# Mixer A's queries and keys turned by transposing DMA transfers of half-word planes instead of TensorE

## The chip, the core and the metric

The kernel runs on one core of one Trainium2 chip. The core has five engines that work side by side, each through its own list of instructions in order: TensorE (PE; matrix products and transposes, results in PSUM), VectorE (DVE), ScalarE (ACT), GpSimd (POOL) and SyncE (SP), which here only issues DMA transfers. They meet through semaphores: an instruction waits until another engine or a transfer has counted far enough. The metric is the device time of one run, in microseconds (us); lower is better. The kernel before takes 1428.91 us (median of 3 runs, 1428.28 to 1428.96).

## What is computed

A two-layer encoder trunk on 512 positions of width 1024, float32. Layer 1 uses mixer A, dilated window attention, layer 2 uses mixer B, latent attention; each is followed by a squared-ReLU MLP of width 4096. What matters here is the front of mixer A: one projection gives queries, keys and values for 3 groups of 8 heads of width 128; queries and keys are RMS-normalised per head and rotated, and then each group takes scores inside its window.

```
def dilated_mixer(h, w_qkv, q_gain, k_gain, w_o):
    qkv = (h @ w_qkv).reshape(B, S, 3, N_GROUPS, A_HEADS, A_HEAD_DIM)
    for g, (window, dil) in enumerate(DIL_CONFIGS):
        q = rope(rms_norm(qkv[:, :, 0, g], q_gain[g]), S)
        k = rope(rms_norm(qkv[:, :, 1, g], k_gain[g]), S)
        v = qkv[:, :, 2, g]
        o, lse = dilated_group(q, k, v, window, dil)
    ...
def reference(x, ...):
    for i in range(DEPTH):
        y = dilated_mixer(...) if i % 2 == 0 else mla_mixer(...)
        x = x + y
        x = x + sq_relu_mlp(rms_norm(x, norm_ffn[i]), ffn_w1[i], ffn_w2[i])
```

The score of a query and a key is a sum over the head's 128 columns. TensorE sums over partitions, so queries and keys must lie with the head's columns on the partitions, while the projection leaves them with the positions there. They have to be transposed in between.

## The kernel before

The 512 positions are cut into 4 chunks of 128 (r = 0 to 3; a chunk holds every fourth position). Mixer A goes over 4 head pairs b, and within each over the groups g = 0, 1, 2. One pair and group make a block: 512 projected columns (two heads of queries, two of keys) for each of the 4 chunks, so there are 12 blocks and 48 chunks.

*Projection.* `qk_proj` runs `run_block` over 8 slices of 128 rows of the weights. Float32 products are made of three matmuls of split operands: `load_unit` reads a weight tile `raw` (L145), ScalarE rounds it to `whi` (L157), VectorE makes the rest `wlo` (L158), and L185 multiplies. Four PSUM banks `acc` hold the four chunks. `raw` has 3 buffers, `whi` and `wlo` 4 each.

*A finished chunk.* `qk_evac` squares the four heads' columns with their sums on ScalarE (L137, `junk` and `qss`), multiplies by cosines into `t1` (L277) and by sines into `t2` (L280), raises the sums to the power -1/2 on GpSimd (L132, `qrs`), adds `t2` to `t1` (L285) and scales `t1` (L286). Then TensorE transposes the four 128x128 pieces of `t1` into one PSUM bank `tp` (L124), and ScalarE copies that bank into `qkT` (L295): into a contiguous slice for groups 1 and 2, into every fourth column for group 0. `t1`, `t2`, `tp` and `qkT` have two buffers each.

*After it.* `scores` (L576, L580, L587) multiplies slices of `qkT`; VectorE adds the mask and takes the maxima (L583, L592, L595, L596), ScalarE takes the exponentials (L598); `merge` weighs the three groups and `pv` multiplies with the values.

*What sets the order.* The code issues blocks one after the other, but the instructions of each engine are put in order by the framework's scheduler when the program is built, from its own estimate of times; on the chip each engine then keeps that order. The order therefore changes in many places of mixer A when the code of one step changes. SP's list holds loads of weights, of the values (`vt`, `v0n`, `v0c`) and of a few constants in this stage.

The lines that the change touches are L263 to L301 (`qk_evac`, `qk_proj`) and L711 to L716 (`project_in`).

Of the kernel before, what the change touches and what calls it, by code (L numbers as in the profile page):

```python
# [9 lines left out]

F32 = mybir.dt.float32
F32R = mybir.dt.float32r
AF = mybir.ActivationFunctionType
ALU = mybir.AluOpType
AX = mybir.AxisListType
# [2 lines left out]
P = 128  # L18
S = 512
NT = S // P  # L20
# [67 lines left out]
def encoder_kernel(ctx: ExitStack, tc: tile.TileContext, x, norm_mix, norm_ffn, a_w_qkv, a_q_gain, a_k_gain,  # L88
                   a_w_o, b_w_in, b_q_a_gain, b_w_qb, b_kv_a_gain, b_w_kvb, b_q_gain, b_k_gain, b_w_o,
                   ffn_w1, ffn_w2, consts, out):  # L90
    nc = tc.nc
    V, A, G, PE = nc.vector, nc.scalar, nc.gpsimd, nc.tensor
# [3 lines left out]
    def nm(s):  # L96
        uid[0] += 1
        return f"{s}_{uid[0]}"
# [14 lines left out]
    tp_p = ctx.enter_context(tc.tile_pool(name="tp_p", bufs=2, space=PSUM))  # L113
# [6 lines left out]
    ident = ck[:, C_ID:C_ID + P]  # L120
    A.activation(warm, nhalf[:, 0:1], AF.Exp)

    def transpose(o, i):
        PE.transpose(o, i, ident)  # L124

    def rstd_of(ss, n, add, name, out=None):

        v = st.tile([P, 8], F32, tag="rs_v", name=nm("rs_v"))
        V.tensor_scalar(v[:, :n], ss, add, None, op0=ALU.add)  # L129
        if out is None:  # L130
            out = st.tile([P, 8], F32, tag=name, name=nm(name))[:, :n]
        G.tensor_tensor(out, v[:, :n], nhalf[:, :n], op=ALU.pow)  # L132
        return out

    def mean_square(junk, x, dim, out):

        A.activation(junk, x, AF.Square, scale=1.0 / math.sqrt(dim), accum_out=out)  # L137

# [11 lines left out]
    def load_unit(src, nk, dims, n, home=None, raw=None):  # L150
# [3 lines left out]
        if home is None:  # L154
            home = [wp.tile([P, 2, 512], F32R, tag=t, name=nm(t)) for t in ("whi", "wlo")]
        hi, lo = home
        A.activation(hi[:, :nk, :n], raw[:, :nk, :n], AF.Copy)  # L157
        V.tensor_tensor(lo[:, :nk, :n], raw[:, :nk, :n], hi[:, :nk, :n].bitcast(F32), op=ALU.subtract)  # L158
# [36 lines left out]
    def run_block(units, groups, n, mm, evac, outs=NT, halves=1):  # L195
        for end in block_groups(units, groups, n, mm, outs, halves):
            if end is not None:
                evac(*end)

    def act_stationary(hT, n):  # L200

        def mm(r, kt, hi, lo, hv):
            ah = hT[:, kt, 0, r * P:(r + 1) * P]
            al = hT[:, kt, 1, r * P:(r + 1) * P]
            sl = slice(0, n)
            return [(ah, hi[:, :n], sl), (ah, lo[:, :n], sl), (al, hi[:, :n], sl)]
        return mm
# [6 lines left out]
    def norm_tile(r, src, gain_b, hT, pool, xn_bufs=2, xn_tag="xn"):  # L214
# [6 lines left out]
        for half in range(2):  # L221
# [5 lines left out]
            tv = tp.rearrange("p (k t) -> p k t", k=4)  # L227
            A.activation(hi, tv, AF.Copy)
            V.tensor_tensor(lo, tv, hi.bitcast(F32), op=ALU.subtract)
# [6 lines left out]
    def new_hT():  # L236
        return big.tile([P, KD, 2, S], F32R, tag="hT", name=nm("hT"))

# [6 lines left out]
    def qk_units(b, g):  # L245
        return [(w6[:, k:k + 2, 0:2, g, 256 * b:256 * b + 256], 2, 2) for k in range(0, KD, 2)]
# [9 lines left out]
    def tables(g, gqk, cos, sin):  # L256

        for t in range(2):
            gb = gqk[:, t].rearrange("p (f d) -> p f d", f=2).unsqueeze(1).broadcast_to([P, NT, 2, 64])
            V.tensor_tensor(cosg[g][:, :, t].rearrange("p r (f d) -> p r f d", f=2),  # L260
                            cos.rearrange("p (r d) -> p r d", r=NT).unsqueeze(2).broadcast_to([P, NT, 2, 64]), gb,
                            op=ALU.mult)
            V.tensor_tensor(sing[g][:, :, t].rearrange("p r (f d) -> p r f d", f=2),  # L263
                            sin.rearrange("p (r f d) -> p r f d", r=NT, f=2), gb, op=ALU.mult)

    def qk_evac(g, qkT, r, acc, homes, junk):

        a4 = acc.rearrange("p (c d) -> p c d", c=4)
        a5 = acc.rearrange("p (t h d) -> p t h d", t=2, h=2)
        ss = st.tile([P, 8], F32, tag="qss", name=nm("qss"))  # L270
        jk = junk()
        for c in range(4):
            mean_square(jk, a4[:, c], DH, ss[:, c:c + 1])
        t1, t2 = homes()
        t15 = t1.rearrange("p (t h) d -> p t h d", t=2)
        t25 = t2.rearrange("p (t h) d -> p t h d", t=2)
        V.tensor_tensor(t15, a5, cosg[g][:, r].unsqueeze(2).broadcast_to([P, 2, 2, DH]), op=ALU.mult)  # L277
        for hf in range(2):
            o_ = 64 - hf * 64
            V.tensor_tensor(t25[:, :, :, hf * 64:hf * 64 + 64], a5[:, :, :, o_:o_ + 64],  # L280
                            sing[g][:, r, :, o_:o_ + 64].unsqueeze(2).broadcast_to([P, 2, 2, 64]), op=ALU.mult)
        rs = rstd_of(ss[:, 0:4], 4, EPS, "qrs")

        def end():
            V.tensor_tensor(t1, t1, t2, op=ALU.add)  # L285
            V.tensor_tensor(t1, t1, rs.unsqueeze(2).broadcast_to([P, 4, DH]), op=ALU.mult)  # L286
            tp = tp_p.tile([P, 512], F32, tag="tp", name=nm("tp"))
            for c in range(4):
                transpose(tp[:, c * P:(c + 1) * P], t1[:, c])
            tv = tp.rearrange("p (c t) -> p c t", c=4)  # L290
            if g == 0:
                dst = qkT.rearrange("p c (m r) -> p c m r", r=NT)[:, :, :, r]
            else:
                dst = qkT[:, :, r * P:(r + 1) * P]
            A.activation(dst, tv, AF.Copy)  # L295
        return end

    def qk_proj(b, g, qkT, homes, junk):

        run_block(qk_units(b, g), [2, 2], 512, act_stationary(hT, 512),  # L300
                  lambda r, acc: qk_evac(g, qkT, r, acc, homes, junk)())  # L301

    def load_gains(g, gqk):
        for t, src in enumerate((a_q_gain, a_k_gain)):
# [2 lines left out]
    def v_phase(vp):  # L307
# [10 lines left out]
        xts = x16.tile([P, NT, D], F32, tag="x16", name="xts")  # L318
        Ssp = [vp.tile([P, 4, 2, 256], F32R, name=f"Ssp{n}") for n in range(4)]

# [42 lines left out]
        def turn(r):  # L363

            i = r % 2
            for half in (1, 0):
# [5 lines left out]
                hi, lo = (hT[:, sl, c, r * P:(r + 1) * P] for c in range(2))  # L372
                A.activation(hi, tv, AF.Copy)
                V.tensor_tensor(lo, tv, hi.bitcast(F32), op=ALU.subtract)
# [28 lines left out]
        def split_w(x):  # L403
            hi = wp.tile([P, 2, 512], F32R, tag="whi", name=nm("whi"))[:, :, :VH]
            lo = wp.tile([P, 2, 512], F32R, tag="wlo", name=nm("wlo"))[:, :, :VH]
            A.activation(hi, x, AF.Copy)
            V.tensor_tensor(lo, x, hi.bitcast(F32), op=ALU.subtract)  # L407
            return hi, lo
# [135 lines left out]
    with tc.tile_pool(name="apool", bufs=1, reuse_waits="tile") as ap_, \  # L544
# [160 lines left out]
        def homes():  # L705
            return [aw.tile([P, 4, DH], F32, tag=t, name=nm(t)) for t in ("t1", "t2")]

        def junk():
            return aw.tile([P, P], F32, tag="junk", name=nm("junk"), bufs=1)

        def project_in(b, g):  # L711
            if b == 0 and g:
                tables(g, gqk[:, g - 1], ca[:, 0:256], ca[:, 256:768])
            qkT = aw.tile([P, 4, S], F32, tag="qkT", name=nm("qkT"))
            qk_proj(b, g, qkT, homes, junk)
            return qkT  # L716

        def finish(b, Pt, stats, vs):
# [3 lines left out]


        qkT = project_in(0, 0)
        for b in range(HA // 2):
            Pt = [[ap_.tile([P, NT, 256 if g == 0 else P], F32, tag=f"P{g}{h}", name=nm("P")) for h in range(2)]
                  for g in range(NG)]
            stats = [st.tile([P, NG, 2, NT], F32, tag=f"stat{j}", name=nm("stat"), bufs=2) for j in range(3)]
            vs = v_load(b)
            for g in range(NG):  # L730
                scores(b, g, qkT, Pt, stats)
                if g + 1 < NG:
                    qkT = project_in(b, g + 1)
            if b + 1 < HA // 2:
                qkT = project_in(b + 1, 0)
                finish(b, Pt, stats, vs)
# [18 lines left out]
    def split_a(x, pool):  # L755
        t = pool.tile([P, 4, 2, 256], F32R, tag="asp", name=nm("asp"), bufs=4)
        A.activation(t[:, :, 0], x, AF.Copy)
        V.tensor_tensor(t[:, :, 1], x, t[:, :, 0].bitcast(F32), op=ALU.subtract)
        return t
# [191 lines left out]
    if True:  # L951
        with tc.tile_pool(name="bpool", bufs=1, reuse_waits="tile") as bp, \
# [208 lines left out]
            for s_ in range(HB * NT + lag):  # L1161
                p, c = divmod(s_, 8)
# [4 lines left out]
                if s_ >= lag:  # L1167
                    d, h2, r2, f = pend.pop(0)
# [58 lines left out]
```

## Time and profile before

| | before |
|---|---|
| median of 3 runs | 1428.91 us |
| span of the profiled execution, first to last instruction | 1425.8 us |
| VectorE busy | 939.6 us, 66% |
| GpSimd busy | 217.2 us, 15% |
| bytes moved by DMA | 185.25 MB |

The profiled execution's own time is its span; the medians are of other runs and include some us around the span. The profile names an instruction by its line, engine, operation, and output and input tiles (`qkT<-tp`). "Busy" is time in which the engine executes. PEld is the loading of TensorE's weights, which overlaps its products. The chain that ended last is followed back from the last instruction to what released it, and so on. In a row of a group, the numbers behind the first bar are busy us and mean ns, those behind the second the idle time just before the instructions, with what ended most of it. SPq stands for SP's queue of DMA issues.

### The profile page before, as it was taken

How to read it: one execution, taken by the hardware profiler on the slowest of the kernel's cores; microseconds unless marked ns; L12 is line 12 of the kernel's file. 1: busy time of each engine (PE TensorE's matmuls, PEld its weight loads, DVE VectorE, ACT ScalarE, POOL GpSimd, SP SyncE). 2: the span in 40 equal slices, each digit the busy share in tenths (PEclk: the TensorE clock that was granted, in tenths of full speed). 3: DMA queues.
4: the chain of work that ended last, by engine and by line, in shares of the span. 5: the costliest groups of instructions: out<-in, count | busy, mean ns of one | idle time of the engine just before them, and what ended most of it. 6: DMA issues, size and time to landing. Idle time of an engine off the chain costs nothing.

```text
span 1425.8 us, 19234 instructions
## 1 busy us (share of the span) xinstructions
PE 1394.0 (98%) x7044; PEld 1183.8 (83%) x7044; DVE 939.6 (66%) x1497; ACT 740.5 (52%) x1594; POOL 217.2 (15%) x240
## 2 busy tenths in 40 slices
PE   7999999999999999999999999999999999999998
PEld 7999888988888988888888887777768888888886
DVE  6886768676886754465564759788745365575647
ACT  6554656464564623553545446677633553544543
POOL 1110212021112001020010203433201020020201
PEclk9999999999999999999999999999999999999999
DMA  9535222322322335668493844200115658394835
GB/s 323 166 134 168 75 87 87 107 89 75 118 61 77 121 134 195 174 133 222 116 233 99 206 120 91 82 31 30 44 40 163 183 127 231 93 234 128 192 90 118
DMA packets 121086, 185.25 MB, mean 130 GB/s; under 512 B 8416, under 2 KB 58336, under 8 KB 120992
## 3 DMA queue, kind: packets, MB, share of 16 engines
q1 hardware_dynamic: 101808, 144.96, 31.6%
q0 software_dynamic: 19184, 39.07, 15.2%
q8 instruction: 55, 0.90, 0.3%
q14 instruction: 39, 0.32, 0.1%
HBM read 176.13 MB, written 7.86 MB: 129 GB/s over the span
## 4 chain that ended last, share of the span: by engine, by line
PE 89%; DVE 6%; ACT 2%; issue 1%; DMA 1%; POOL 0%; SPq 0%; DVEq 0%; ACTq 0%; POOLq 0%
PE acc L185 51%; PE sc L852 11%; PE tp L852 7%; PE tp L124 4%; PE sc L421 3%; PE acc L1138 1%; PE sc L1032 1%; PE acc L1114 1%; PE tp L421 1%; DVE wlo L796 1%; PE sco L701 1%; PE sc L587 1%; PE acc L421 1%; PE sco L697 1%; DVE wlo L407 1%
## 5 line engine op out<-in xcount | busy, mean ns | idle before, releaser
L185 PE MATMUL acc<-whi,hT 128*128 128x512 f32 (+2 forms) x1216 | 384.2, 390 | 2.2 <-ACT hT L739 1.3
L185 PE MATMUL acc<-hT_f,whi 128*128 128x512 f32 (+1 forms) x1152 | 318.7, 366 | 1.7 <-DVE resid L915 1.2
L158 DVE TENSOR_TENSOR wlo<-raw,whi 128x1024 fp32r<-128x1024 f32 (+3 forms) x146 | 172.4, 1189 | 180.2 <-ACT whi L157 179.9
L185 PEld LDWEIGHTS acc<-whi,hT 128*128 128x128 f32 x1216 | 225.4, 188 | 42.0 <-ACT hT L739 1.9
L185 PEld LDWEIGHTS acc<-hT_f,whi 128*128 128x128 f32 x1152 | 208.1, 189 | 37.4 <-DVE resid L915 1.6
L185 PE MATMUL acc<-wlo,hT 128*128 128x512 f32 (+2 forms) x608 | 235.9, 388 | 0.0
L157 ACT ACTIVATE whi<-raw 128x1024 fp32r<-128x1024 f32 (+3 forms) x146 | 149.7, 1031 | 161.5 <-PE acc L185 64.1
L796 DVE TENSOR_TENSOR wlo<-wqs,whi 128x1024 fp32r<-128x1024 f32 x112 | 137.9, 1232 | 113.4 <-ACT whi L795 113.4
L185 PE MATMUL acc<-hT_f,wlo 128*128 128x512 f32 (+1 forms) x576 | 204.9, 366 | 0.0
L795 ACT ACTIVATE whi<-wqs 128x1024 fp32r<-128x1024 f32 x112 | 118.8, 1061 | 161.3 <-PE acc L185 65.8
L852 PE MATMUL sc<-whi,asp 128*128 128x512 f32 x512 | 164.9, 390 | 0.8 <-DVE resid L826 0.7
L781 POOL DMA_DIRECT2D wqs<-in_ffn_w_dram x64 | 77.6, 1344 | 546.1 <-DVE wlo L796 362.4
L185 PEld LDWEIGHTS acc<-wlo,hT 128*128 128x128 f32 x608 | 114.4, 188 | 18.7 <-issue 0.2
L185 PEld LDWEIGHTS acc<-hT_f,wlo 128*128 128x128 f32 x576 | 108.5, 189 | 17.4
L852 PE MATMUL tp<-whi,asp 128*128 128x512 f32 x352 | 112.2, 390 | 1.8 <-DVE resid L826 1.8
L852 PEld LDWEIGHTS sc<-whi,asp 128*128 128x128 f32 x512 | 96.1, 188 | 21.4 <-issue 1.5
L132 POOL TENSOR_TENSOR qrs<-rs_v,nhalf 128x4 f32<-128x4 f32 x48 | 58.7, 1228 | 288.8 <-DVE rs_v L129 239.7
L852 PE MATMUL sc<-wlo,asp 128*128 128x512 f32 x256 | 99.6, 389 | 0.0
L137 ACT ACTIVATE junk<-acc 128x128 f32<-128x128 f32 x192 | 53.0, 276 | 56.4 <-PE acc L185 51.4
L852 PEld LDWEIGHTS tp<-whi,asp 128*128 128x128 f32 x352 | 66.1, 188 | 16.4 <-DVE resid L826 2.7
L852 PE MATMUL tp<-wlo,asp 128*128 128x512 f32 x176 | 68.2, 389 | 0.0
L295 ACT ACTIVATE qkT<-tp 128x512 f32<-128x512 f32 x48 | 35.8, 765 | 51.2 <-PE tp L124 50.9
(231 smaller groups left out, 2185.3 us busy)
## 6 DMA issues: line engine op xcount, KB each, us to landing
wqs<-in_ffn_w_dram SPq DMA_DIRECT2D x80, 512.0 KB, 5.1
raw<-in_ffn_w_dram SPq DMA_DIRECT2D x64, 512.0 KB, 4.5
wqs<-in_ffn_w_dram POOLq DMA_DIRECT2D x64, 512.0 KB, 7.5
raw<-in_a_w_qkv_dram SPq DMA_DIRECT2D x96, 256.0 KB, 3.1
b<-in_a_w_qkv_dram SPq DMA_DIRECT2D x24, 384.0 KB, 5.7
vall<-vo POOLq DMA_DIRECT2D x24, 192.0 KB, 2.2
raw<-in_a_w_o_dram SPq DMA_DIRECT2D x8, 512.0 KB, 3.8
raw<-in_b_w_o_dram SPq DMA_DIRECT2D x8, 512.0 KB, 3.7
```

The source lines that it names most:

```text
L124: PE.transpose(o, i, ident)
L132: G.tensor_tensor(out, v[:, :n], nhalf[:, :n], op=ALU.pow)
L137: A.activation(junk, x, AF.Square, scale=1.0 / math.sqrt(dim), accum_out=out)
L157: A.activation(hi[:, :nk, :n], raw[:, :nk, :n], AF.Copy)
L158: V.tensor_tensor(lo[:, :nk, :n], raw[:, :nk, :n], hi[:, :nk, :n].bitcast(F32), op=ALU.subtract)
L185: PE.matmul(accs[o][:, oc], lhsT=lt, rhs=rt, start=(kt == 0 and p_i == 0 and hv == 0), stop=(kt == total - 1 and p_i == 2), skip_group_che ...
L295: A.activation(dst, tv, AF.Copy)
L421: PE.matmul(banks[t][:, :VH], lhsT=lt, rhs=rt[:, j], start=(first and k == 0 and i_ == 0), stop=(k == 3 and i_ == 2), skip_group_check=True)
L781: marks["sum"] = nc.gpsimd.dma_start(t, src, accum_op=ALU.add).ins
L795: A.activation(hi, x, AF.Copy)
L796: V.tensor_tensor(lo, x, hi.bitcast(F32), op=ALU.subtract)
L852: PE.matmul(bk[t], lhsT=lt, rhs=rt[:, j], start=(first and k == 0 and i_ == 0), stop=(k == 3 and i_ == 2), skip_group_check=True)
```

## The change

The transposes of `t1` on TensorE and the PSUM bank `tp` are taken out of `qk_evac`. In their place:

1. ScalarE copies `t1`, read as 16-bit words, into `t2` as two planes of 512 words per partition: all lower halves, then all upper halves (`halves`). `t2`'s float contents have been added to `t1` by then.
2. SP issues one transposing transfer per chunk, from `halves` (128 partitions x 1024 words) into a new tile `xT` (128 x 8 x 128 words, two buffers): eight blocks of 128x128 words, each transposed.
3. ScalarE copies `xT` into `qkT`, the lower and upper half of each word beside each other again.

```
-    def qk_evac(g, qkT, r, acc, homes, junk):
+    def qk_evac(g, qkT, r, acc, homes, junk, turned):
...
             V.tensor_tensor(t1, t1, t2, op=ALU.add)
             V.tensor_tensor(t1, t1, rs.unsqueeze(2).broadcast_to([P, 4, DH]), op=ALU.mult)
-            tp = tp_p.tile([P, 512], F32, tag="tp", name=nm("tp"))
-            for c in range(4):
-                transpose(tp[:, c * P:(c + 1) * P], t1[:, c])
-            tv = tp.rearrange("p (c t) -> p c t", c=4)
+            halves = t2.rearrange("p c d -> p (c d)").bitcast(U16)
+            A.activation(halves.rearrange("p (h n) -> p h n", h=2),
+                         t1.rearrange("p c d -> p (c d)").bitcast(U16).rearrange("p (n h) -> p h n", h=2), AF.Copy)
+            xT = turned()
+            nc.sync.dma_start_transpose(xT, halves)
             if g == 0:
-                dst = qkT.rearrange("p c (m r) -> p c m r", r=NT)[:, :, :, r]
+                dst = qkT.bitcast(U16).rearrange("p c (m r h) -> p c m r h", r=NT, h=2)[:, :, :, r]
             else:
-                dst = qkT[:, :, r * P:(r + 1) * P]
-            A.activation(dst, tv, AF.Copy)
+                dst = qkT[:, :, r * P:(r + 1) * P].bitcast(U16).rearrange("p c (m h) -> p c m h", h=2)
+            A.activation(dst, xT.rearrange("p (h c) t -> p c t h", h=2), AF.Copy)
...
+        def turned():
+            return aw.tile([P, 8, P], U16, tag="xT", name=nm("xT"))
```

The scheduler's order changes with it. Lines of the changed kernel are one higher from L13 on, two higher behind `qk_evac`'s end and five higher behind `turned`: the square is L138, the weight split L158, the first copy L289, the transfer L292, the copy back L297, the scores L578, L582 and L589.

ScalarE, from the squares of the very first block on (names with t are `t1` and `t2`), before:

```order
L137 ACTIVATE junk_1326,qss_1325<-acc_1233 128x128 x4
L137 ACTIVATE junk_1361,qss_1360<-acc_1234 128x128 x4
L137 ACTIVATE junk_1396,qss_1395<-acc_1235 128x128 x4
L157 ACTIVATE whi_1590<-raw_1587 128x1024
L137 ACTIVATE junk_1431,qss_1430<-acc_1236 128x128
L157 ACTIVATE whi_1597<-raw_1594 128x1024
L137 ACTIVATE junk_1431,qss_1430<-acc_1236 128x128 x3
L295 ACTIVATE qkT_1232<-tp_1342 128x512
```

and at the same place in the changed kernel:

```order
L138 ACTIVATE junk_1392,qss_1391<-acc_1235 128x128 x3
L289 ACTIVATE t_183_1332<-t_182_1331 128x1024
L138 ACTIVATE junk_1392,qss_1391<-acc_1235 128x128
L158 ACTIVATE whi_1582<-raw_1579 128x1024
L289 ACTIVATE t_190_1365<-t_189_1364 128x1024
L138 ACTIVATE junk_1425,qss_1424<-acc_1236 128x128
L158 ACTIVATE whi_1589<-raw_1586 128x1024
L297 ACTIVATE qkT_1232<-xT_1343 128x512x2
L138 ACTIVATE junk_1425,qss_1424<-acc_1236 128x128
L297 ACTIVATE qkT_1232<-xT_1376 128x512x2
```

Two instructions per chunk stand where one stood, and squares and splits of later chunks stand between and behind them.

SP, the loads of the weights of the following blocks, before:

```order
L145 DMA raw_1774<-in_a_w_qkv_dram 128x2x256 x2
L145 DMA raw_1781<-in_a_w_qkv_dram 128x2x256 x2
L145 DMA raw_1836<-in_a_w_qkv_dram 128x2x256 x2
L145 DMA raw_1843<-in_a_w_qkv_dram 128x2x256 x2
L145 DMA raw_2019<-in_a_w_qkv_dram 128x2x256 x2
```

and now:

```order
L146 DMA raw_1758<-in_a_w_qkv_dram 128x2x256 x2
L292 DMA_TRANSPOSE xT_1343<-t_183_1332 128x8x128
L292 DMA_TRANSPOSE xT_1376<-t_190_1365 128x8x128
L146 DMA raw_1765<-in_a_w_qkv_dram 128x2x256 x2
L146 DMA raw_1820<-in_a_w_qkv_dram 128x2x256 x2
L292 DMA_TRANSPOSE xT_1409<-t_197_1398 128x8x128
L292 DMA_TRANSPOSE xT_1442<-t_204_1431 128x8x128
L146 DMA raw_1827<-in_a_w_qkv_dram 128x2x256 x2
```

The same loads stand in the same sequence, with the transfers of the finished chunks between them.

TensorE, around the first scores of the second block, before (`sc_1741` and `sc_1753` are the two heads' score banks):

```order
L185 MATMUL acc_1770<-whi_1784,hT_91 128x512
L185 MATMUL acc_1771<-whi_1777,hT_91 128x512
L124 MATMUL tp_1665<-ck,t_250_1654 128x128 x4
L587 MATMUL sc_1741<-qkT_1520 128x128
L587 MATMUL sc_1753<-qkT_1520 128x128
L185 MATMUL acc_1771<-wlo_1778,hT_91 128x512
```

and now, where the last scores of that block stand:

```order
L186 MATMUL acc_1756<-whi_1823,hT_91 128x512 x2
L589 MATMUL sc_1725<-qkT_1512 128x128
L589 MATMUL sc_1737<-qkT_1512 128x128
L186 MATMUL acc_1756<-wlo_1824,hT_91 128x512
L186 MATMUL acc_1756<-whi_1823,hT_91 128x512
```

The transposes are gone from the list, and the scores stand further behind the projection that they need: before, the first pair stands among the opening matmuls of the next block's first two banks; now the last pair stands in the second half of the next block.

More of the change, by code (lines that the diff above doesn't have):

```diff
@@ L12 @@
 F32R = mybir.dt.float32r
+U16 = mybir.dt.uint16
 AF = mybir.ActivationFunctionType
@@ L286, in end, with qk_proj @@
             V.tensor_tensor(t1, t1, rs.unsqueeze(2).broadcast_to([P, 4, DH]), op=ALU.mult)
-            tp = tp_p.tile([P, 512], F32, tag="tp", name=nm("tp"))
-            for c in range(4):
-                transpose(tp[:, c * P:(c + 1) * P], t1[:, c])
-            tv = tp.rearrange("p (c t) -> p c t", c=4)
+            halves = t2.rearrange("p c d -> p (c d)").bitcast(U16)
[3 more added lines that the diff above has]
+            nc.sync.dma_start_transpose(xT, halves)
             if g == 0:
-                dst = qkT.rearrange("p c (m r) -> p c m r", r=NT)[:, :, :, r]
+                dst = qkT.bitcast(U16).rearrange("p c (m r h) -> p c m r h", r=NT, h=2)[:, :, :, r]
             else:
-                dst = qkT[:, :, r * P:(r + 1) * P]
-            A.activation(dst, tv, AF.Copy)
+                dst = qkT[:, :, r * P:(r + 1) * P].bitcast(U16).rearrange("p c (m h) -> p c m h", h=2)
+            A.activation(dst, xT.rearrange("p (h c) t -> p c t h", h=2), AF.Copy)
         return end
-    def qk_proj(b, g, qkT, homes, junk):
+    def qk_proj(b, g, qkT, homes, junk, turned):
         run_block(qk_units(b, g), [2, 2], 512, act_stationary(hT, 512),
-                  lambda r, acc: qk_evac(g, qkT, r, acc, homes, junk)())
+                  lambda r, acc: qk_evac(g, qkT, r, acc, homes, junk, turned)())
     def load_gains(g, gqk):
@@ L714, in project_in @@
             qkT = aw.tile([P, 4, S], F32, tag="qkT", name=nm("qkT"))
-            qk_proj(b, g, qkT, homes, junk)
+            qk_proj(b, g, qkT, homes, junk, turned)
             return qkT
```

## The prediction

> **What bounds the kernel now.** I read the page first: the busy shares, then the chain that ended last.
>
> ```profile
> span 1425.8 us, 19234 instructions
> ...
> PE 1394.0 (98%) x7044; PEld 1183.8 (83%) x7044; DVE 939.6 (66%) x1497; ACT 740.5 (52%) x1594; POOL 217.2 (15%) x240
> ...
> PE 89%; DVE 6%; ACT 2%; issue 1%; DMA 1%; POOL 0%; SPq 0%; DVEq 0%; ACTq 0%; POOLq 0%
> ```
>
> TensorE is busy for 98% of the span and is 89% of the chain. The changed code runs only in mixer A's attention, so the next view is the busy time of each engine from the first to the last copy into `qkT`, and the chain from 140 to 490 us.
>
> ```profile
> core 0: us, PE busy (x) PEld busy (x) DVE busy (x) ACT busy (x) POOL busy (x), PEclk, DMA share, GB/s
> 148.80:482.90 334.10, 334.10 (x1868) 289.05 (x1867) 244.17 (x494) 184.18 (x636) 54.87 (x45) 1.00 0.28 87
> ```
>
> ```profile
> by line: PE acc L185 75.8%; PE tp L124 9.0%; PE sc L587 4.1%; PE sco L697 3.1%; PE sco L701 3.1%; PE sc L580 2.0%; PE sc L576 2.0%; PE scm L642 0.7%; PE scm L667 0.3%
> ```
>
> In these 334.1 us TensorE never idles and the chain is TensorE alone, at full clock. So every microsecond taken from it is a gain as long as nothing else becomes late. ScalarE is busy for 184.2 us, 55%. Those two numbers carry the whole argument: TensorE gets shorter, and ScalarE, through which the replacement goes twice, gets longer.
>
> **What is removed from TensorE.** The groups say how many transposes there are, the timeline what four of them cost.
>
> ```profile
> L124 PE MATMUL tp<-ck,t x192: 270/272/275, 148.2 to 481.9; 128*128 128x128 f32 x192
> ```
>
> ```profile
> 147.70 0.62 PE L185 MATMUL acc<-whi,hT 128*128 128x512 f32 x2
> 148.16 0.60 PE L124 MATMUL tp<-ck,t 128*128 128x128 f32 x4
> 148.51 0.48 PE L185 MATMUL acc<-wlo,hT 128*128 128x512 f32 x1
> 148.83 0.63 PE L185 MATMUL acc<-whi,hT 128*128 128x512 f32 x2
> ```
>
> ```profile
> 217.51 6.82 PE acc L185 x30
> ```
>
> The 0.272 us of one transpose is a pipelined duration, so 192 of them are not 52 us. A projection matmul takes 6.82/30 = 0.227 us in a row. After the two that begin at 147.70, the next two would begin at 148.16 and 148.39; with four transposes between they begin at 148.51 and 148.83, which is 0.44 us late. 48 groups of four make 48 x 0.44 = **21 us** off TensorE: its floor for the stage falls from 334 to 313 us.
>
> **What is added to ScalarE.** Its ledger of the stage, by line, with busy time, mean of one, and idle time before:
>
> ```profile
> L137 ACT ACTIVATE junk<-acc 128x128 f32<-128x128 f32 x176 | 48.6, 276 | 55.1 <-PE acc L185 50.5 <-issue 1.1
> L157 ACT ACTIVATE whi<-raw 128x1024 fp32r<-128x1024 f32 x41 | 43.1, 1056 | 10.6 <-PE acc L185 10.2
> L295 ACT ACTIVATE qkT<-tp 128x512 f32<-128x512 f32 x48 | 35.8, 765 | 51.2 <-PE tp L124 50.9
> L137 ACT ACTIVATION_READ_ACCUMULATOR junk<-acc 128x1 f32 x176 | 34.4, 195 | 0.0
> ...
> L598 ACT ACTIVATE P<-P,stat 128x256 f32<-128x256 f32 x32 | 15.9, 500 | 6.1 <-DVE stat L596 6.1
> L690 ACT ACTIVATE pT<-tp 128x512 f32<-128x512 f32 x12 | 7.2, 598 | 26.1 <-PE tp L124 26.1
> ```
>
> ```profile
> L295 ACT ACTIVATE qkT<-tp x48: 577/599/1157, 148.8 to 482.3; 128x512 f32<-128x512 f32 x48
> ```
>
> The copy into half-word planes writes 1024 elements per partition. The nearest row is the 1024-element split `whi`, 1.056 us: 48 x 1.056 = 50.7 us. The copy back has 1024 elements too, 50.7 us, and replaces 35.8 us. So ScalarE's work is 184.2 + 50.7 + 50.7 - 35.8 = 249.8 us. No row shows 16-bit operands. Half the price (two to a cycle) would take 50 us off; against it stands the strided case: the old copy takes 0.60 us into contiguous columns and up to 1.16 us where group 0 writes every fourth column, so a strided write can double. If the 16 copies back of group 0 double, 16.9 us come on top: 266.7 us. I take 250 to 267 and keep the halved price only for the low end, where TensorE's floor holds anyway.
>
> **The wait that the change puts on ScalarE.** The copy back waits for the transfer, and ScalarE works in order. Behind it stand the squares of the next chunks (which free `acc` banks), the weight splits, and the exponentials. Landing times of transfers of the same and of smaller size:
>
> ```profile
> raw<-in_a_w_qkv_dram SPq DMA_DIRECT2D x96, 256.0 KB, 3.1
> ...
> out_dram<-resid SPq DMA_DIRECT2D x8, 256.0 KB, 2.0
> ...
> g_mix<-in_norm_mix_dram SPq DMA_DIRECT2D x2, 512.0 KB, 11.9
> ```
>
> ```profile
> L606 SPq DMA_DIRECT2D v0c<-vall x32: 445/594/602, 268.8 to 497.9; - x32
> ```
>
> A transposing transfer isn't in the trace. It moves 256 KB, so 2.0 us is the low end, and the slow broadcast of 11.9 us the far end. I take 3.1 us, the row of the same size, queue and stage, plus one issue ahead of it on SP (0.594 us): **3.7 us** from the end of the first copy to the landing. To see how much of this ScalarE fills with other work I laid its new order end to end with the durations above. Between a first copy and its copy back it has 0 to 12.6 us of other work, in 25 of 48 cases under 3 us, in 14 under 1.5 us. This makes ScalarE wait 14 us in all at 2 us, 34 at 3.1, 49 at 3.7, 79 at 4.7 and 103 at 5.5. These are estimates from the rows, not rows.
>
> The sum for ScalarE: 249.8 + 49 + 10.6 (its present wait for weight buffers, which I keep) = 309; at the dear end 266.7 + 48 + 10.6 + 6.9 (its waits for the maxima) = 332. Its other waits (50.5 and 26.1 us) are for TensorE and shrink when ScalarE is the late one. The middle is **321 us**, 8 above TensorE's 313. So the stage goes from 334 to 321: 13 us of the 21 stay.
>
> **What else is touched.** The scores wait for the copies back. In the new TensorE order 76 projection matmuls and 14 small ones stand between the last projection matmul of the first group-1 block (chunk 3) and that chunk's own scores: 76 x 0.227 alone is 17 us.
>
> ```profile
> L132 POOL TENSOR_TENSOR qrs<-rs_v,nhalf 128x4 f32<-128x4 f32 x47 | 57.2, 1223 | 272.6 <-DVE rs_v L129 223.5 <-DVE stat L596 20.4 <-DVE me L668 16.4
> ...
> L286 DVE TENSOR_TENSOR t<-t,qrs 128x512 f32<-128x512 f32 x48 | 32.6, 683 | 2.8 <-POOL qrs L132 2.4
> ```
>
> The chain from a finished chunk is four squares with the reads of their sums (0.28 + 0.20 us each, 1.9), the power on GpSimd 1.2, the product 0.7, the copy 1.06, the transfer 3.7, the copy back 1.06: 9.6 us. It fits with 7 us left; without that cover each of the 12 blocks would pay the difference. `t2` now stays occupied until the transfer has read it, and has two buffers: about 8 us for two chunks, 4 us each, 16 for the four of a block, of the 313/12 = 26 us that TensorE takes per block. On SP, weight loads stand behind transposes that wait for ScalarE.
>
> ```profile
> SPq L145 <- DVE wlo L158: 200.0, 33, 16.3
> ```
>
> SP waits 200 us of the stage for VectorE to free a raw buffer, so loads go out as early as buffers allow and two transposes ahead of one can be absorbed; I cost this at nothing. VectorE's and GpSimd's work is unchanged. After the attention stage the order on all engines is as before.
>
> **The sum.** 1425.8 - 13 = 1412.8 us by the span; the median of the runs shown, 1428.9, lies 3.1 us above the span. That gives **1416 us**, with a range of its own of 1410 to 1425.
>
> **Rivals.** *TensorE stays the bound.* If landing takes 2 to 3 us, ScalarE needs at most 250 + 34 + 11 = 295 us and the whole 21 us stay: 1408 us. For it: the plain 2.0 us store and the halved 16-bit price. Against: transposing can only add to a plain transfer. Chance 0.17.
>
> *ScalarE's wait becomes the bound, and the kernel is slower.* ScalarE without its transfer waits is (249.8 + 266.7)/2 + 14 = 272 us, so it passes 334 us when those waits reach 62 us, by the steps above at 4.1 us from copy to landing. At 4.7 us the stage is 272 + 79 = 351, the kernel 1446 us; at 5.5 us 375, and 1470. The place is the copy back (L297 of the changed kernel), with squares and splits queued behind it. For it: 4.1 is only 0.4 above my value, and many weight loads share the queue. Against: the 256 KB rows of 2.0 and 3.1 us. Chance 0.25.
>
> *The wait just eats the saving*: 1426 to 1432 us, around 4.1 us. Chance 0.10.
>
> *The eight 128-column blocks of a transfer go one after the other.* Bounded by eight issues of 0.594 us on top of 3.1, a transfer lands after 7.9 us; the waits, growing by about 32 us per us, are then 180 us, the stage 272 + 180 = 452 and the kernel 1547 us; bounded by eight full small landings it is far more. Nothing in the trace speaks for this, and no row excludes it. Chance 0.08.
>
> The Trainium skill has a rule against the change: "VectorE: DVE Perf Modes", section "The three transpose paths", lists 1309 ns for a crossbar DMA transpose of one 128x128 bf16 block and 390 ns for TensorE. TensorE's f32 transposes here show 272 ns, less than that page gives; by its DMA figure eight blocks in a row would be an estimated 10.5 us per transfer and 48 of them 503 us of queue, some 170 us over the present stage, which is the last rival. No row of this trace decides it.
>
> That the change does nothing of what it says I leave out: in the built order the 192 transposes are gone and 48 transfers are there.
>
> **How the numbers follow.** Forecast 0.40, TensorE-bound 0.17, eaten 0.10, slower by the wait 0.25, block by block 0.08. A difference under 0.2%, 2.9 us, can't be told from none here. Faster is 0.40 + 0.17 = 0.57, the same 0.10, slower 0.33. The range starts at 1407, TensorE's floor, and runs to 1452, which takes in most of the slower case (4.9 us to landing) and leaves out its tail and the block-by-block case, about 0.17.
>
> **What will show it.** The stage between the first and last copy into `qkT`: 321 us, or 313, or over 334. Landing of `xT`: 3.7 us, decision at 4.1. Copies of 16-bit elements: 1.06 us each, in group 0 up to 2.1. ScalarE's waits for `xT`: about 49 us in all. TensorE should show idle time of some 8 us before scores or `acc` banks. I am wrong if TensorE idles on weights (SP's queue), or if the copies aren't near 1.06 us.

## The result and the profile after

| | before | after |
|---|---|---|
| median | 1428.93 us, 4 runs (1428.28 to 1429.52) | 1413.97 us, 4 runs (1412.54 to 1415.63) |
| ratio, 95% interval | | 0.9895 (0.9883 to 0.9907) |
| span of the profiled execution | 1425.8 us | 1412.0 us |

The kernel became 15.0 us faster. First the page of the kernel after: its span, the busy shares, the shares of the chain that ended last, and the group of the copy back.

```profile
span 1412.0 us, 18967 instructions
...
PE 1374.6 (97%) x6852; PEld 1166.0 (83%) x6852; DVE 940.3 (67%) x1497; ACT 801.3 (57%) x1642; POOL 225.9 (16%) x240
...
PE 80%; DVE 7%; ACT 5%; DMA 4%; issue 2%; POOL 1%; SPq 0%; DVEq 0%; ACTq 0%; POOLq 0%
...
L297 ACT ACTIVATE qkT<-xT 128x1024 uint16<-128x1024 uint16 x48 | 56.5, 1182 | 42.5 <-DMA xT<-t 42.2
```

TensorE's share of the chain fell from 89% to 80%; transfers rose from 1% to 4%, ScalarE from 2% to 5%. The kernel is still TensorE's, but the chain now leaves it at places. The next view is the stage from the first to the last copy into `qkT`, as for the kernel before: busy time and instructions of each engine, TensorE's clock, share of DMA and GB/s.

```profile
150.40:465.50 315.10, 311.75 (x1668) 268.60 (x1667) 244.64 (x493) 241.84 (x674) 62.23 (x46) 1.00 0.55 133
```

The stage takes 315.1 us where it took 334.1. ScalarE is busy for 241.8 us instead of 184.2, and TensorE, which never idled here, now idles for 315.10 - 311.75 = 3.35 us. The tile `xT` of the kernel after says how long issue, landing and copy back take (ns, min/median/max), and who waits for the transfer; the row behind it is the copy into planes.

```profile
L292 SPq DMA_TRANSPOSE xT<-t x48: 1232/1238/1897, 147.0 to 460.3; - x48
L297 ACT ACTIVATE qkT<-xT x48: 1161/1184/1202, 150.4 to 464.3; 128x1024 uint16<-128x1024 uint16 x48
...
  ACT qkT L297: 42.2, 29
  DVE t L281: 11.6, 9
...
DMA to landing us min/median/max: 3.0/3.2/5.7
```

```profile
L289 ACT ACTIVATE t<-t x48: 1039/1048/1064, 146.0 to 456.7; 128x1024 uint16<-128x1024 uint16 x48
```

A transfer lands 3.2 us after its issue, and ScalarE stood still for 42.2 us in all waiting for one, in 29 of the 48 cases. VectorE waited 11.6 us before a product with sines for a `t2` that a transfer was still reading. What reaches TensorE is in its own waits, from 140 to 540 us (in all, times, longest):

```profile
PE acc L186 <- ACT hT L744: 3.7, 2, 2.3
PE sco L703 <- ACT pT L692: 1.6, 1, 1.6
PE sc L589 <- ACT qkT L297: 1.6, 1, 1.6
```

Of 42.2 us on ScalarE, TensorE feels 1.6 at a score and some more through ScalarE's backlog: the waits for `hT` and `pT` are for ScalarE too. In the kernel before, the wait for `hT` is the only one of these, and smaller:

```profile
PE acc L185 <- ACT hT L739: 1.3, 2, 1.0
```

Where the longest of these waits comes from, the chain shows at the end of the stage (start, us, what):

```profile
458.90 4.31 DMA xT<-t
...
464.33 1.17 ACT qkT L297
465.50 0.95 ACT whi L158
...
467.42 2.11 ACT P L600 x11
...
470.90 1.54 ACT P L600 x8
...
475.37 0.53 ACT hT L744
...
475.94 1.18 PE acc L186 x4
```

The last block has no later projection of queries and keys to hide behind. Its last transfer ends late, ScalarE still has the exponentials of that block to do, and only then makes `hT`, for which the output projection's first product, at 475.94 us, waits 2.3 us, the longest wait of the kernel after's list. In the kernel before that product started at 491.16. So 15.2 us are gained at that point. Of the stage's 19.0 us, 1.6 were used up as it began later (150.4 against 148.8), 2.2 behind it. By the end of the program 13.8 are left by the spans.

### The profile page after: what moved, and what is told of

Its sections match the earlier page's. It is cut to its first block, busy times and chain, and to the rows that moved or that the text cites. A ratio compares the mean times of both kernels' runs of the same rounds, so it can differ in the third digit from the quotient of the medians.

```text
span 1412.0 us, 18967 instructions
## 1 busy us (share of the span) xinstructions
PE 1374.6 (97%) x6852; PEld 1166.0 (83%) x6852; DVE 940.3 (67%) x1497; ACT 801.3 (57%) x1642; POOL 225.9 (16%) x240
## 4 chain that ended last, share of the span: by engine, by line
PE 80%; DVE 7%; ACT 5%; DMA 4%; issue 2%; POOL 1%; SPq 0%; DVEq 0%; ACTq 0%; POOLq 0%
PE acc L186 46%; PE sc L857 11%; PE tp L857 7%; PE sc L423 3%; DMA xT<-t 3%; PE tp L125 3%; PE acc L1143 1%; PE sc L1037 1%; PE acc L1119 1%; PE tp L423 1%; DVE wlo L801 1%; PE acc L423 1%; DVE wlo L159 1%; PE sco L703 1%; PE sc L589 1%
## 5 line engine op out<-in xcount | busy, mean ns | idle before, releaser
L186 PE MATMUL acc<-whi,hT 128*128 128x512 f32 (+2 forms) x1216 | 378.7, 388 | 4.6 <-ACT hT L744 3.7
L158 ACT ACTIVATE whi<-raw 128x1024 fp32r<-128x1024 f32 (+3 forms) x146 | 149.3, 1028 | 154.0 <-PE acc L186 61.6
L133 POOL TENSOR_TENSOR qrs<-rs_v,nhalf 128x4 f32<-128x4 f32 x48 | 66.5, 1388 | 262.7 <-DVE rs_v L130 233.8
L297 ACT ACTIVATE qkT<-xT 128x1024 uint16<-128x1024 uint16 x48 | 56.5, 1182 | 42.5 <-DMA xT<-t 42.2
L831 DVE TENSOR_TENSOR resid<-resid,sc 128x512 f32<-128x512 f32 x64 | 43.1, 682 | 25.6 <-PE sc L857 25.6
```

What stands on the lines that cost most here:

```text
L186: PE.matmul(accs[o][:, oc], lhsT=lt, rhs=rt, start=(kt == 0 and p_i == 0 and hv == 0), stop=(kt == total - 1 and p_i == 2), skip_group_che ...
L297: A.activation(dst, xT.rearrange("p (h c) t -> p c t h", h=2), AF.Copy)
L831: V.tensor_tensor(sl, sl, banks[t], op=op)
```

## The experiments

All are edits of the kernel after. The scheduler makes a new order for each of them, so a variant never differs from the kernel after by its edit alone. Theory A, from the profile: TensorE's relief is worth its whole 21 us, and a part is given back where a transfer's landing shows through ScalarE's ordered list. Rivals: the two added copies cost it, being work on ScalarE; or SP's queue does, in which 48 issues hold up the loads.

Two numbers are given beside each time, as they turned out to explain most of the spans: TensorE's idle time between 140 and 540 us (400 less its busy time there), and the time lost to a lower granted clock (over slices of 10 us, TensorE's busy time times one less the clock, summed, the last slice of the span left out). Both, like the span, are of the one profiled execution of each kernel. Each ratio is to the kernel before on the same chip and in the same series.

| kernel | median us (range) | ratio to before (95%) | span | TensorE idle | lost to clock |
|---|---|---|---|---|---|
| before | 1428.5 to 1429.0 | 1 | 1425.8 | 1.7 | 0.0 |
| after | 1414.0 (1412.5 to 1415.6) | 0.9895 (0.9883 to 0.9907) | 1412.0 | 8.3 | 1.3 |
| e10_copies_alone | 1428.8 (1427.5 to 1430.2) | 0.9998 (0.9989 to 1.0007) | 1427.7 | 1.7 | 1.5 |
| e1_dead_transposes | 1439.8 (1437.9 to 1443.4) | 1.0081 (1.0066 to 1.0097) | 1436.1 | 8.3 | 1.6 |
| e7_no_transfer | 1406.2 (1405.2 to 1406.3) | 0.9842 (0.9827 to 0.9856) | 1403.5 | 2.9 | 0.0 |
| e2_twice | 1456.8 (1454.6 to 1461.1) | 1.0201 (1.0181 to 1.0221) | 1453.2 | 31.5 | 9.0 |
| e4_issue_from_ScalarE | 1444.0 (1438.1 to 1446.6) | 1.0106 (1.0087 to 1.0125) | 1441.7 | 23.7 | 8.7 |
| e5_planes_on_GpSimd | 1410.7 (1409.6 to 1411.8) | 0.9872 (0.9857 to 0.9887) | 1409.7 | 6.2 | 1.3 |
| e8_planes_on_VectorE | 1421.2 (1418.2 to 1422.9) | 0.9944 (0.9932 to 0.9957) | 1420.8 | 10.6 | 5.6 |
| e6_group0_back | 1422.2 (1421.3 to 1424.2) | 0.9958 (0.9945 to 0.9970) | 1422.3 | 7.0 | 4.2 |
| e3_third_t2 | 1420.7 (1418.4 to 1422.5) | 0.9944 (0.9928 to 0.9961) | 1418.6 | 11.4 | 1.4 |
| e9_GpSimd_third_t2 | 1416.7 (1416.3 to 1416.9) | 0.9912 (0.9899 to 0.9926) | 1414.5 | 8.6 | 4.2 |

**What the copies, the transfers and TensorE's relief are each worth.** Three variants make a square with the kernel after: TensorE's transposes there (into a bank that nobody reads) or not, transfers there or not, both copies always there. The two without transfers leave the transposition out of queries and keys, so their output isn't the reference's.

```
e7_no_transfer
-            xT = turned()
-            nc.sync.dma_start_transpose(xT, halves)
-            A.activation(dst, xT.rearrange("p (h c) t -> p c t h", h=2), AF.Copy)
+            A.activation(dst, halves.rearrange("p (h c t) -> p c t h", h=2, c=4), AF.Copy)
e1_dead_transposes
+            tp = tp_p.tile([P, 512], F32, tag="tp", name=nm("tp"))
+            for c in range(4):
+                transpose(tp[:, c * P:(c + 1) * P], t1[:, c])
e10_copies_alone: both edits
```

> The changed kernel, with the 192 TensorE transposes put back as extra work into a PSUM bank that nobody reads; the transfers still feed the scores. If the gain is TensorE's shorter list, 48 x 0.44 = 21 us come back, less some waits that the extra work now covers: 1427 to 1436 us. If the gain comes from the new order of the other engines, or from ScalarE no longer waiting for the transposes, the time stays within 5 us of 1414.

> The transfers and xT are left out; the copy back reads the planes as they are, so queries and keys are not transposed and the output is not the reference's. TensorE, the copies and all else stay. If the transfer's latency costs what was given back of the 21 us, 1406 to 1410 us. If the give-back is in ScalarE's two copies, no change: 1412 to 1415.

> TensorE's 192 transposes stay, into a bank that nobody reads; both copies of 1024 half words stay on ScalarE; the transfers are left out and the copy back reads the planes, so queries and keys aren't transposed and the output isn't the reference's. If the copies' work (66 us more on ScalarE) costs nothing by itself and only the landing does, this gives the time of the kernel before, 1428.5 us, within 2. If the copies are the part that made the variant with dead transposes and transfers 11 us slower than before, it gives 1435 or more.

| median us | TensorE's transposes stay | gone |
|---|---|---|
| without transfers | 1428.75 | 1406.17 |
| with transfers | 1439.80 | 1413.97 |

The copies alone give 1428.75 us, the time of the kernel before (interval 0.9989 to 1.0007): as was expected: they cost nothing that can be measured. TensorE's relief is worth 22.6 us without transfers and 25.8 with them. The transfers cost 7.8 us beside the relieved TensorE and 11.1 beside the other. So 15 us are 22.6 less 7.8, or 25.8 less 11.1, within 0.3. The kernel without transfers came out at the lower edge of its expected 1406 to 1410. The one with dead transposes was expected at 1427 to 1436 us and took 1439.8: the extra work was to cover some of the transfers' waits, and they cost 3.3 us more there instead. That the copies cost nothing, the rows of busy time from 140 to 540 us show directly, first for the kernel before, then for the copies alone:

```profile
140.00:540.00 400.00, 398.26 (x2216) 344.46 (x2215) 283.70 (x563) 212.83 (x716) 59.25 (x49) 1.00 0.30 94
```

```profile
140.00:540.00 400.00, 398.27 (x2215) 344.38 (x2214) 284.38 (x563) 273.81 (x765) 59.12 (x49) 1.00 0.30 94
```

ScalarE works 61.0 us more, and TensorE is busy for the same time. In the kernel without transfers TensorE's largest wait in this stretch is the one that the kernel before has too, 1.3 us for `hT`; that wait, and the row:

```profile
PE acc L186 <- ACT hT L742: 1.3, 2, 1.0
```

```profile
140.00:540.00 400.00, 397.07 (x2166) 344.15 (x2165) 299.89 (x583) 284.80 (x779) 71.72 (x54) 1.00 0.33 104
```

The same row of the kernel after has the same ScalarE, 283.48 us against 284.80, and 5.4 us less of TensorE's busy time:

```profile
140.00:540.00 400.00, 391.68 (x2105) 337.26 (x2104) 296.10 (x579) 283.48 (x780) 68.37 (x52) 1.00 0.51 130
```

The rival that ScalarE's added work costs the time falls here. The 7.8 us of the transfers appear in the spans as 1412.0 - 1403.5 = 8.5 us, of which 5.4 are TensorE's idle time in this stretch and 1.3 the lower clock. They hold what the scheduler's new order does as well as what the landing does; the square doesn't part the two.

**More latency.** The second transfer repeats the first in the same queue.

```
+            nc.sync.dma_start_transpose(xT, halves)
```

> Each transposing transfer is done twice in series into the same tile, so the landing takes about 6.4 us instead of 3.2 and SP is held 1.24 us more. If the wait on ScalarE decides from about 4 us on, as predicted, the saving is gone and more: 1425 to 1470 us (the scheduler, which knows of the second transfer, will put more work between, so rather the lower half). If the transfer is hidden with room to spare, 1414 to 1418.

ScalarE's longest waits in the stage, the tile's rows, and TensorE's two longest waits from 140 to 540 us:

```profile
ACT qkT L298 <- DMA xT<-t: 75.5, 37, 5.1
```

```profile
L292 SPq DMA_TRANSPOSE xT<-t x48: 1231/1236/2085, 146.0 to 501.1; - x48
L293 SPq DMA_TRANSPOSE xT<-t x48: 1231/1232/1458, 149.6 to 504.3; - x48
...
  DVE t L281: 39.5, 22
```

```profile
PE sc L590 <- ACT qkT L298: 7.6, 6, 2.9
PE sco L704 <- ACT pT L693: 5.4, 3, 3.9
```

The second issue follows the first by 3.6 us, so each chunk's path is that much longer. The time rises by 42.8 us where the first transfer cost 7.8, and TensorE idles 31.5 us, longest before scores that wait for a copy back. The time lies in the range of 1425 to 1470, though not in its lower half as expected. So the cost grows steeply with the second transfer. A likely reason is that the cover is used up: ScalarE idles 315.1 - 241.8 = 73 us in the stage of the kernel after, and a first round trip, 48 x 3.2 = 154 us in all, leaves only 42 us of waiting there, and few of these reach TensorE; with a second the reserve is gone. The edit doesn't isolate the latency, though: a second transfer also holds SP for 1.23 us more per chunk, and VectorE waits 39.5 us for `t2` where it waited 11.6.

**Where the transfer is issued.**

```
-            nc.sync.dma_start_transpose(xT, halves)
+            nc.scalar.dma_start_transpose(xT, halves)
```

> The same transfers are issued from ScalarE's queue instead of SP's. If what costs time is the hold on SP (weight loads and value loads queued behind 48 holds of 1.24 us and behind the waits for the copy into planes), the kernel becomes faster than 1414 us, towards 1407. If ScalarE's own order is the place (theory A), the hold of 1.24 us moves to the engine that is the late one: 48 x 1.24 = 59 us more on ScalarE, which was busy 242 and idle 73 of 315 us in the stage and waited 42 us of these for xT, so part of the hold lies inside those waits: 1414 + 10 to 30 us, about 1430.

The hold of 1.25 us goes to ScalarE's list, and the kernel is 30 us slower than after, at the far end of the 10 to 30 expected:

```profile
L292 ACTq DMA_TRANSPOSE xT<-t x48: 1247/1248/1498, 145.6 to 488.6; - x48
```

Its transfers have a queue of their own in this run (packets, MB, share of 16 engines' span):

```profile
q10 hardware_dynamic: 50688, 12.59, 5.2%
```

With SP free of transposes TensorE idled 23.7 us, not less, so the hold costs far more on ScalarE's list than on SP's. A small gain on SP could hide in that loss; against it speaks that TensorE hardly ever waits for weights in the kernel after (0.2 us, shown further down).

**Where the copy into planes runs.**

```
-            A.activation(halves.rearrange("p (h n) -> p h n", h=2), t1..., AF.Copy)
+            G.tensor_copy(halves.rearrange("p (h n) -> p h n", h=2), t1...)      e5_planes_on_GpSimd
+            V.tensor_copy(halves.rearrange("p (h n) -> p h n", h=2), t1...)      e8_planes_on_VectorE
```

> The copy into half-word planes goes to GpSimd. ScalarE loses 48 x 1.05 = 50 us of work. If ScalarE's work is what costs (rival), the time falls to 1407 to 1410 us. If the landing that shows in ScalarE's in-order queue is what costs (theory A), ScalarE reaches its copy back sooner and waits longer for xT: its waits rise from 42 to 60 us or more and the time stays at 1411 to 1418; a GpSimd copy that takes over 2 us adds its excess to each chunk and makes it slower, 1420 or more.

> The copy into half-word planes goes to VectorE, right behind the product that it copies, so one hop between engines falls out of the chain of each chunk and ScalarE loses 50 us of work. VectorE is busy 245 of the stage's 315 us; a copy of 1.1 us makes that 298, of 0.7 us 279. Theory A: the chain from product to landing is shorter by the time that the copy stood in ScalarE's queue, so a part of the 8 us comes back: 1408 to 1413 us. Rival (VectorE becomes the late engine, as ScalarE is now): 1415 to 1425 us, with ScalarE waiting for VectorE and TensorE for acc banks.

On GpSimd the copy takes as long as on ScalarE, and ScalarE's waits for `xT` rise, since it reaches its copy back sooner. First the copy, then ScalarE's waits from 140 to 500 us:

```profile
L289 POOL COPY t<-t x48: 1030/1040/3102, 145.6 to 464.2; 128x1024 uint16<-128x1024 uint16 x48
```

```profile
ACT qkT L297 <- DMA xT<-t: 72.5, 28, 7.5
ACT P L600 <- DVE stat L598: 19.5, 11, 3.8
```

50 us of work left ScalarE, 30 us of waiting for `xT` came in, and the kernel gained 3.2 us: 1410.7 lies between the two ranges, 0.3 below theory A's and 0.7 above the rival's. It is the fastest of those that compute the whole result, by little: its runs and those of the kernel after do not overlap (1411.8 at most against 1412.5 at least), but the intervals of their ratios do, by a hair (0.9857 to 0.9887 against 0.9883 to 0.9907). On VectorE the copy is shorter, yet the kernel is slower than after by 7.2 us; the copy, and ScalarE's waits from 140 to 490 us:

```profile
L289 DVE COPY t<-t x48: 677/684/694, 146.0 to 474.1; 128x1024 uint16<-128x1024 uint16 x48
```

```profile
ACT qkT L297 <- DMA xT<-t: 72.6, 27, 8.1
ACT P L600 <- DVE stat L598: 29.9, 11, 4.5
```

ScalarE waits 29.9 us for VectorE's maxima, against 2.9 in the kernel after: VectorE became late, as the rival had it, and the time lies in its range of 1415 to 1425. This isn't the whole cause. The GpSimd variant has 19.5 us of such waits and is fast; TensorE's longest waits here are for copies back (5.1 us in all), not for `acc` banks; and of the 8.8 us between the spans of this variant and the kernel after, 2.3 are idle time and 4.3 a lower clock.

**Only groups 1 and 2.**

```
+            if g == 0:
+                tp = tp_p.tile([P, 512], F32, tag="tp", name=nm("tp"))
...
+                return
```

> Only groups 1 and 2 go through transposing transfers; group 0 has its four TensorE transposes and its one copy back again. Theory A (TensorE's relief of about 0.45 us a chunk, less the latency that shows): 32 of 48 chunks keep both the relief and the cost, so two thirds of the 15 us stay, about 1419 us. Rival B (group 0, whose copy back writes every fourth column and whose block stands first in each round, is where the cost arises): nearly all of the 15 us stay, 1414 us or less, since the 7 us given back to TensorE come with the 8 us of latency saved. Rival C (the cost arises in groups 1 and 2): 1423 us or more.

1422.2 us is between theory A (1419) and rival C (1423). The last columns of the table say why: by the spans it is 3.5 us faster than before, its relief is 32 x 0.44 = 14.1, it idles 5.3 us more than before, and a lower clock takes 4.2. Three slices of the end of its stage, where that clock shows (the column ahead of the last two):

```profile
470.00:480.00 10.00, 7.42 (x39) 6.68 (x38) 5.31 (x7) 8.28 (x16) 0.00 (x0) 0.88 0.46 124
480.00:490.00 10.00, 10.00 (x47) 8.28 (x47) 7.32 (x18) 6.11 (x21) 0.00 (x0) 0.94 0.54 174
...
500.00:510.00 10.00, 8.04 (x45) 7.68 (x46) 3.62 (x5) 1.20 (x2) 0.00 (x0) 0.66 0.83 299
```

So it says nothing against one of the groups; how the cost is shared out among them stays open.

**A third buffer for `t2`**, with the planes copied on ScalarE and on GpSimd.

```
-            return [aw.tile([P, 4, DH], F32, tag=t, name=nm(t)) for t in ("t1", "t2")]
+            return [aw.tile([P, 4, DH], F32, tag=t, name=nm(t), bufs=n) for t, n in (("t1", 2), ("t2", 3))]
```

> t2, which the transfer reads, has three buffers instead of two. This takes away VectorE's 11.6 us of waits for transfers. If what was given back of TensorE's 21 us is lost to other places (a few waits of TensorE for ScalarE), the time stays at 1411 to 1415. If the two buffers cost it, 1407 to 1410.

> Planes copied on GpSimd as before, and t2 with three buffers, so that VectorE's wait for a t2 that a transfer still reads (26.3 us in the stage with two buffers) should fall under 10 us. Theory A (what is left is TensorE's idle time, 6.2 us in 140 to 540 us against 1.7 in the kernel before, plus a dip of the granted clock worth 1.3 us): the time falls by at most these 5 us, 1406 to 1411. Rival (the waits of VectorE cost nothing since something else is late, and a third buffer only makes the planner lay the work out in another order): the time moves by TensorE's idle time of the new order, 1410 to 1420, with no sign foretold.

VectorE's wait for `t2` went, from 11.6 to 2.9 us in the first and from 26.3 to none that its list of waits names in the second, and both kernels became 6 to 7 us slower than with two buffers. The first, 1420.7, lies outside both of its ranges; the second, 1416.7, in the rival's. VectorE's waits with two buffers on GpSimd's variant, and with three on ScalarE's:

```profile
DVE t L281 <- DMA xT<-t: 26.3, 14, 4.6
```

```profile
DVE t L281 <- DMA xT<-t: 2.9, 1, 2.9
```

So the time doesn't follow this wait. The scheduler laid out all engines but GpSimd anew with the third buffer on ScalarE's variant, and TensorE idles 11.4 us instead of 8.3. Why the new order is the worse one was not followed further. It means that some 6 to 7 us of any of these variants can be the order's. So the 3.2 us of the GpSimd variant can't be put down to ScalarE's relief, the 7.2 of VectorE's can't be put down to VectorE alone, and of the 7.8 us that the transfers cost, the part of the landing itself stays open.

**The spans put together.** If 22.6 us of relief (14.1 for e6) is the gain, idle time and clock the loss, the spans of all but e2 and e4 come out within 4.5 us (no relief for e1 and e10): the kernel after, 1425.8 - 22.6 + (8.3 - 1.7) + 1.3 = 1411.1 against 1412.0; GpSimd's variant, 1409.0 against 1409.7; VectorE's, 1417.7 against 1420.8; the worst, the third buffer, 1414.3 against 1418.6. For e2 and e4 the sum gives 1442.0 and 1433.9 against 1453.2 and 1441.7. There some 8 to 11 us are missing; the ends of matmuls in TensorE's busy time are modelled and may hide them, which was not followed further.

## The prediction, step by step

- **TensorE loses 48 x 0.44 = 21 us.** Right: 22.6 by the two kernels without transfers.
- **ScalarE's work is 250 to 267 us in the stage.** It was 241.8 between the two limits, but only because other work moved out of them: from 140 to 540 us ScalarE's busy time rose by 70.7 us, where the sum added 65.6 to 82.5. The copy into planes was right (1.06, measured 1.05), the copy back dearer in all groups (1.06, measured 1.18), and the doubling in group 0 didn't come: the slowest copy of all took 1.20 us.
- **3.7 us from the copy's end to the landing.** The first one took 150.4 - 147.05 = 3.35 us, the landing from the issue a median of 3.2. I had added an issue of 0.594 us ahead of 3.1. The hold on SP is 1.24 us, twice that, but it lies inside the landing.
- **ScalarE waits 49 us for `xT`.** 42.2; by the steps given, 34 at 3.1 and 49 at 3.7, that is a landing of 3.4. The slope beyond it was too steep: with a second transfer in series the path is 3.6 us longer and the waits rose by 33 us, not by some 115 (32 us per us). I had held the order fixed, and the scheduler didn't: in ScalarE's list of the kernel after 4.6 other instructions stand between a copy into planes and its copy back on average, with the second transfer 7.6 (reads of sums and copies of other chunks not counted). The point from which it turns slower, 4.1 us, was not reached, so it is untested as a number; the 1456.8 us with two transfers suggest that there is such a point.
- **ScalarE's sum of work and waits, 321 us, sets the stage.** The stage took 315.1, and this is the step that failed as reasoning. I made ScalarE the bound by adding work to waits, so that any work taken from it had to be a gain. The copies alone cost nothing, and of 50 us taken off ScalarE 30 came back as waiting for `xT`. What TensorE waits for is a few late handovers, the longest at the stage's end. The 13 us kept by the prediction and the 13.8 by the spans agree, but through another split: 19.0 gained in the stage, 5.2 lost around it. That the forecast of 1416 us came within 2 us of the measured 1414.0 is therefore in part luck.
- **TensorE idles some 8 us, before scores or `acc` banks.** 8.3 us between 140 and 540, right in size; the largest piece, 3.7, is before the output projection, which I had not named.
- **Loads behind transposes on SP cost nothing.** Right: TensorE's only wait for weights in the stage is 0.2 us (below), and ScalarE waited 2.4 us for them.

```profile
PE acc L186 <- DVE wlo L159: 0.2, 1, 0.2
```

- **`t2` fits in two buffers.** Not quite: VectorE waited 11.6 us. That these cost time was not shown; without most of them the kernel was slower, in another order.
- **TensorE stays the bound, 1408 us.** Not quite: TensorE is still the longest part of the chain, but the kernel after lies 6 us above this figure. The kernel without transfers, 1406.2, is its floor, and the GpSimd variant lies 4.6 above that. **The blocks of a transfer one after another, 1547 us.** It fell: eight blocks of 128 columns land in 3.2 us.

  The Trainium skill's page "VectorE: DVE Perf Modes", section "The three transpose paths", with 1309 ns for one bf16 block of 128x128, would have made an estimated 10.5 us of them; the trace differs, and its 3.2 us decide.

## What to carry to other kernels

Here the step that left the bounding engine gave its full price there (22.6 us against 21 reckoned), and what it cost elsewhere was not the work (61 us more on ScalarE cost nothing by themselves) but the round trip: count how much other work stands behind the sender's copy at each chunk, the last one above all, before counting busy shares. Don't let the receiving engine hold for the issue, which cost 30 us here. Moving its other work away helped little (3.2 us on GpSimd, 15% busy) or hurt (7.2 us lost on VectorE, 66% busy), and neither is clear of what a new order alone can do. Where a scheduler lays out the order, read idle time and granted clock of the bounding engine in each variant before a few microseconds are put down to the edit.

## What was unexpected of the hardware

- A transposing transfer of 256 KB from SBUF to SBUF lands in 3.2 us, as long as a plain load of that size takes in the stage, though it is cut small: 50688 packets for 48 transfers are 1056 each, some 248 bytes. It holds its issuing queue for 1.24 us, where a load holds it for some 0.4 to 0.6. The kernel after, from 140 to 480 us:

```profile
raw<-in_a_w_qkv_dram SPq DMA_DIRECT2D x80, 256.0 KB, 3.2
xT<-t SPq DMA_TRANSPOSE x48, 3.2
```

  Whether it slows its neighbours is not shown. The 512 KB gathers of `v0n` landed in 7.1 us instead of 5.6 in the kernel before, but the kernel without transfers has 7.4:

```profile
v0n<-vall SPq DMA_DIRECT2D x3, 512.0 KB, 7.4
```

- The copy of 1024 half words takes 1.05 us on ScalarE and 1.04 on GpSimd; on VectorE it takes 0.68, as long as a float32 copy of 512 elements out of PSUM takes there (L685, 0.68). So the halved price for 16-bit operands is seen on VectorE alone.
- TensorE's granted clock falls to half for a while after short idle stretches. In the kernel after, later in the program, where the order is the one of before, a slice of 10 us has 0.83; finer slices of 3.41 us show what it is made of:

```profile
1070.00:1080.00 10.00, 7.92 (x44) 6.88 (x44) 8.44 (x10) 5.71 (x9) 0.57 (x2) 0.83 0.67 226
```

```profile
1072.05:1075.46 3.41, 1.87 (x12) 1.23 (x10) 3.41 (x5) 2.24 (x5) 0.00 (x0) 1.00 0.59 157
1075.46:1078.87 3.41, 2.87 (x14) 2.87 (x15) 2.75 (x5) 0.60 (x1) 0.55 (x1) 0.50 1.05 402
1078.87:1082.28 3.41, 3.41 (x31) 3.41 (x31) 2.14 (x3) 1.66 (x2) 0.74 (x1) 1.00 1.01 356
```

  The clock is half for 3.41 us and full on both sides. Other dips have this length or two or three times it, as in the end of e6's stage, twice:

```profile
501.59:508.42 6.83, 6.14 (x30) 5.75 (x29) 1.51 (x3) 1.20 (x2) 0.00 (x0) 0.50 0.97 356
```

  In the kernel without transfers the same work with the same idle time kept the full clock:

```profile
1060.00:1070.00 10.00, 7.92 (x46) 6.47 (x45) 8.44 (x12) 7.13 (x11) 1.10 (x2) 1.00 0.41 147
```

  So idle time alone doesn't tell whether a dip comes; what else decides stays open. Up to 9 us of these kernels' spans are lost to such dips. The Trainium skill's page "TensorE: Matmul & The Clock Gate", Part 1, tells of a free-running window of about 3.4 us and a half clock after an idle one. The length and the half agree with the rows; that a whole window must be idle does not: the slice of 10 us idles for 2.08 us in all, and TensorE was busy for 1.87 of the 3.41 us ahead of the dip.
